# Convolution taps, map differences and RoPE on VectorE in a two-layer hybrid attention block

## The chip, the cores and the metric

The kernel runs on one core of one Trainium2 chip. The metric is the device time of one execution in microseconds (us), the median of several runs. A core has five engines with queues of their own: PE (TensorE, matmuls; its weight loads are listed as PEld), DVE (VectorE), ACT (ScalarE), POOL (GpSimd) and SP (SyncE, which issues the DMAs here). PE writes its results to PSUM; everything else lies in SBUF.

## The reference, cut to what matters

512 latent tokens and 256 context tokens of width 1024 go through two layers. A layer normalises and modulates its input, projects it to 2560 columns in one combined projection, and computes four head groups from that; their outputs are joined, projected and added to the stream, and a SwiGLU feed-forward network follows. The second layer computes no context output. What the change touches:

```python
def apply_rope(x, cos, sin):                      # groups A and C, latent tokens only
    x1, x2 = x[..., :half], x[..., half:]
    return concatenate([x1 * cs - x2 * sn, x1 * sn + x2 * cs])

def conformer_conv(u, w_dw, b_dw, ln_g, ln_b):    # group B: 256 channels
    a, gate = split(u, 2)
    h = a * sigmoid(gate)
    h = depthwise_conv(h, w_dw, taps=31, padding=15) + b_dw
    return silu(layernorm(h, ln_g, ln_b))

def diff_weights(q, k, v, lam):                   # group C: 4 heads, 2 maps each, 32 columns
    p = softmax(q k^T * 32 ** -0.5)
    w = p[map 0] - lam * p[map 1]
    return w @ v
```

Group A is windowed attention with a sink, group D neighbourhood attention on an 8 x 64 grid.

## The kernel before, in words

All matmuls of weights are done in three passes (`mm3`): each operand is held as a high part (fp32r) and a low part, and the products high-high, high-low and low-high are summed in PSUM. A weight tile (`w_unit`) is loaded by SP into one of three raw buffers (wraw), cast to its high part by ACT (whi, L142) and its low part is subtracted by DVE or, for some units, by POOL (wlo, L144). A projection of 128 columns (`unit`) writes the 512 latent tokens and, where needed, the 256 context tokens into the two PSUM buffers pu. While `self.half` is 1 the latent tokens are done as two passes of 256 columns each, behind the context tokens; otherwise as one pass of 512, ahead of them. `self.half` is 1 from the start of group C's attention to the end of group A's projections: in each layer q and k of the second half of group C, q, k and v of group D, and four units of group A.

`rope` (L466) copies a projection out of PSUM on ACT, swaps the halves with a matmul by a permutation (into PSUM, pt), multiplies by sine and cosine on DVE (L474, L475) and adds the two on POOL (L476). There are seven in each layer, four of group C and three of group A.

The convolution (`conv_taps`, L871) runs per half of the channels, 128 channels on the partitions and 783 columns in layer 0 (latent tokens, padding, context) or 512 in layer 1. Of the 31 taps, 20 are formed on ACT as a scaled copy (cpr, L885; the first one, L882, is written to accp directly) and added on POOL (accp, L886); 11 are done on DVE as a multiply and an add in one instruction (accd, L892 and L894). POOL adds both sums at the end (yB, L897). It is a generator: each step is one tap of POOL and about half a tap of DVE, and `mix2` draws steps between those of other generators, in the projections of groups B, C and D. The space of the convolution is given back before the value projections of group D.

`c_attn` (L634) works through blocks of 128 queries and one head: twelve blocks for each of the two head pairs in layer 0 (eight latent ones with 768 keys, four of context with 256), eight in layer 1. A block computes the scores of both maps (sc, L628; there is one score buffer), reduces each to its smallest value while it moves it to SBUF (Pm, nm, L660, DVE), exponentiates on ACT (L663), computes the coefficient (cf, L668, DVE), and takes the weighted difference of the maps: in layer 1 and in every second block of layer 0 as a scaling on ACT (L671) and an addition on POOL (L672), else in one instruction on DVE (L674). The result is transposed on PE (pt, L513) and copied out (PT, L524 on ACT, L527 on DVE); `evac` shares such copies out by the columns given to each engine so far. PE then multiplies by V (L619).

`beside` runs a main generator with a side one between its steps. Group C's first pair runs beside the rest of the projections of group C and the first ones of D, its second pair beside the remaining ones of D.

The program gives an order, and a planner (`schedule_with_timeline_sim=True`) puts the instructions of each engine in their final order by its own costs; each engine then works through its queue in order.

Of the kernel before, what the change touches and what calls it, by code (L numbers as in the profile page):

```python
# [10 lines left out]
AF = mybir.ActivationFunctionType  # L11
ALU = mybir.AluOpType
# [4 lines left out]
P = 128  # L17
D = 1024
NK = D // P
SEQ = 512  # L20
CTX = 256
NT = SEQ + CTX
# [12 lines left out]
QSC_AD = -0.125  # L35
QSC_C = -(32.0 ** -0.5)
CONV_K = 31
CONV_P = 20
PADC = 15
HPW = PADC + SEQ + PADC + CTX + PADC  # L40
ACW = SEQ + PADC + CTX
# [9 lines left out]
class Hybrid:  # L51
# [414 lines left out]
    def rope(self, lat, ct, st, pm, pool):  # L466

        nc = self.nc
        e = self.tl(pool, [P, 512], "rt", 4)
        nc.scalar.copy(e, lat[:, 0:512])  # L470
        sw = self.ps("pt")
        nc.tensor.matmul(sw[:, 0:512], self.perm[:, pm * P:(pm + 1) * P], e, start=True, stop=True)
        v = self.tl(pool, [P, 512], "rt", 4)
        nc.vector.tensor_tensor(v, sw[:, 0:512], self.cs[:, st:st + 512], op=ALU.mult)  # L474
        nc.vector.tensor_tensor(e, e, self.cs[:, ct:ct + 512], op=ALU.mult)  # L475
        nc.gpsimd.tensor_tensor(e, e, v, op=ALU.add)  # L476
        return e

    QKB = 12
# [39 lines left out]
    def evac(self, dst, src):  # L519

        n = int(np.prod(src.shape[1:]))
        if self.load[0] <= self.load[1] * 2.0:
            self.load[0] += n
            self.nc.scalar.copy(dst, src)  # L524
        else:
            self.load[1] += n
            self.nc.vector.tensor_copy(dst, src)  # L527
# [107 lines left out]
    def c_attn(self, l, u):  # L635
        nc = self.nc
        q_ = self.lay[l]
        if u == 0:
            self.nblk = 0
            self.L0 = self.tl(self.cpool, [P, 6, 4], "L0", 1)  # L640
        L0 = self.L0
        Q, K = self.qkc["q", u], self.qkc["k", u]
        for n in range(6 if l == 0 else 4):
            lat = n < 4
            w = NT if lat else CTX
            nb = w // P
            PT = []
            for j in range(2):
                h = 2 * u + j
                rows = [slice(64 * j + 32 * m, 64 * j + 32 * m + 32) for m in range(2)]  # L650
                pss = self.ps2("sc")
                qs = [[a[:, n * P:(n + 1) * P] for a in Q]] * 2
                self.burst_of([f for c0, c1, o in (((0, 512, 0), (512, NT, 512)) if lat else ((512, NT, 0),)) for f in
                               self.mm_rows([ps[:, o:o + c1 - c0] for ps in pss], qs, [[a[:, c0:c1] for a in K]] * 2, rows)])
                Pm = []
                lm = self.small(1, "l1")
                for m in range(2):
                    nm = self.small(1, "nm")
                    Pm.append(self.a_s())
                    nc.vector.tensor_tensor_reduce(out=Pm[m][:, 0:w], in0=pss[m][:, 0:w],  # L660
                                                   in1=self.zcol.to_broadcast([P, w]),
                                                   scale=1.0, scalar=HUGE, op0=ALU.add, op1=ALU.min, accum_out=nm)
                    nc.scalar.activation(Pm[m][:, 0:w], Pm[m][:, 0:w], AF.Exp, scale=-1.0, bias=nm,  # L663
                                         accum_out=L0[:, n, h:h + 1] if m == 0 else lm)
                rl = self.small(1, "rl")
                nc.vector.reciprocal(rl, lm)
                cf = self.small(1, "cf")
                nc.vector.scalar_tensor_tensor(cf, L0[:, n, h:h + 1], q_["nlam"], rl, op0=ALU.mult, op1=ALU.mult)  # L668
                self.nblk += 1
                if l or self.nblk % 2 == 0:  # L670
                    nc.scalar.activation(Pm[1][:, 0:w], Pm[1][:, 0:w], AF.Copy, scale=cf)  # L671
                    nc.gpsimd.tensor_tensor(Pm[0][:, 0:w], Pm[0][:, 0:w], Pm[1][:, 0:w], op=ALU.add)  # L672
                else:
                    nc.vector.scalar_tensor_tensor(Pm[0][:, 0:w], Pm[1][:, 0:w], cf, Pm[0][:, 0:w],  # L674
                                                   op0=ALU.mult, op1=ALU.add)
                PT.append(self.a_pt())
                self.tr_copy([Pm[0][:, b * P:(b + 1) * P] for b in range(nb)], PT[j])
                yield
            self.pv([[(self.VC[:, kb, (2 * u + j) * 64:(2 * u + j) * 64 + 64], self.blk(PT[j], kb - 6 + nb))
                      for kb in range(6 - nb, 6)] for j in range(2)], self.yg["C"][:, u, n * P:(n + 1) * P])  # L680
# [190 lines left out]
    def conv_taps(self, l, pool, u):  # L871
        nc = self.nc
        w = ACW if l == 0 else SEQ
        acc = self.tl(self.cv, [P, ACW], "accd", 1)
        hp = self.hp[u]
        accp = self.tl(self.cv, [P, ACW], "accp", 1)
        nv = CONV_K - CONV_P
        for k in range(CONV_P):
            wc = self.wcol[:, l * 62 + 2 * k + u:l * 62 + 2 * k + u + 1]
            src = hp[:, k:k + w]  # L880
            if k == 0:
                nc.scalar.activation(accp[:, 0:w], src, AF.Identity, scale=wc, bias=self.vcol[:, 2 * l + u:2 * l + u + 1])  # L882
            else:
                pr = self.tl(self.cv, [P, ACW], "cpr", 2)
                nc.scalar.activation(pr[:, 0:w], src, AF.Copy, scale=wc)  # L885
                nc.gpsimd.tensor_tensor(accp[:, 0:w], accp[:, 0:w], pr[:, 0:w], op=ALU.add)  # L886
            for j in range(k * nv // CONV_P, (k + 1) * nv // CONV_P):
                kk = CONV_P + j
                wc = self.wcol[:, l * 62 + 2 * kk + u:l * 62 + 2 * kk + u + 1]
                src = hp[:, kk:kk + w]  # L890
                if j == 0:
                    nc.vector.tensor_scalar(acc[:, 0:w], src, wc, None, op0=ALU.mult)  # L892
                else:
                    nc.vector.scalar_tensor_tensor(acc[:, 0:w], src, wc, acc[:, 0:w], op0=ALU.mult, op1=ALU.add)  # L894
            yield
        for a0, a1, c0 in ((0, SEQ, 0), (SEQ, NT, ACW - CTX))[:1 if l else 2]:
            nc.gpsimd.tensor_tensor(self.yg["B"][:, u, a0:a1], accp[:, c0:c0 + a1 - a0], acc[:, c0:c0 + a1 - a0],  # L897
                                    op=ALU.add)

    def conv_norm(self, l, pool):  # L900
        nc = self.nc
# [102 lines left out]
    def layer(self, l):  # L1004
# [77 lines left out]
        self.cv = self.pool("conv", "left")  # L1082
        self.VC = self.tl(c1, [P, 6, 256], "V", 1)
        self.VA = self.tl(c1, [P, 6, P], "VA", 1)
        self.load = [0, 0]

        def taps():
            for u in range(2):
                yield from self.conv_taps(l, c1, u)
        tp = taps()  # L1090
        for u in range(2):
            for _ in self.mix2(self.proj_b(l, H, c1, u), tp if u else iter(()), 1, False):
                pass
        self.burst, self.ada_tag, self.atags = 0, "pt", [("wraw", 3, F32, self.wst)]
        adas = self.ada_gen([(0, 3)] if l == 0 else [])
        for _ in self.mix2(self.mix2(self.proj_c(l, H, c1, 0), tp, 3, False), adas, 2, False):
            pass
        for _ in adas:
            pass
# [2 lines left out]
        nq = 6 if cx else 4  # L1102

        def d_rest():
            yield from self.mix2(self.proj_d(l, H, c1, 1), tp, 5, False)
            for _ in tp:
                pass
            self.cv.release()
            c2 = held["c2"] = self.pool("mixd", "left")
            self.VD = self.tl(c2, [P, 6, 256], "VD", 1)  # L1110
            self.maskd = self.tl(c2, [P, 768], "mask")
            self.dma(self.maskd, t["maskd"])
            for u in range(2):
                self.v_turned(self.unit(self.w_unit(t["w_in"][l], DV + u * P, True), H, True, "k"), c1,
                              self.VD[:, :, u * P:(u + 1) * P])
                yield
# [11 lines left out]
        def more():  # L1128
# [2 lines left out]
            both = [self.load_wo(l, wo, held["wop"], range(wa)), self.ada_gen([(l, 2)])]  # L1131
            yield from self.chain(*both[::-1 if l else 1])

        self.half = 1
        self.beside(self.c_attn(l, 0), self.mix2(self.chain(self.proj_c(l, H, c1, 1), self.proj_d(l, H, c1, 0)), tp, 4, False),
                    2 * nq, 4)
        self.beside(self.c_attn(l, 1), d_rest(), 2 * nq, 4)
        self.psum_pop()
        self.psum_push("e")
        dn = 10 if cx else 8  # L1140
# [196 lines left out]
def _constants():  # L1337
# [5 lines left out]
    for dim, cc, ss in ((64, C_CA, C_SA), (32, C_CC, C_SC)):  # L1343
        nf = dim // 4
        inv = (np.float32(10000.0) ** (-np.arange(nf, dtype=np.float32) / np.float32(nf))).astype(np.float32)
        ang = np.concatenate([row[:, None] * inv, col[:, None] * inv], axis=1)
        p = np.arange(P)
        idx = p % (dim // 2)
        sgn = np.where(p % dim < dim // 2, -1.0, 1.0).astype(np.float32)
        c[:, cc:cc + SEQ] = np.cos(ang).astype(np.float32).T[idx]  # L1350
        c[:, ss:ss + SEQ] = np.sin(ang).astype(np.float32).T[idx] * sgn[:, None]
        perm[p, 0 if dim == 64 else 1, p ^ (dim // 2)] = 1.0
# [39 lines left out]
```

## Time and profile before

| what | value |
|---|---|
| median of 3 runs | 1831.48 us (1829.79 to 1834.33) |
| profiled execution | 1833.57 us |
| its span, first to last instruction | 1831.8 us |
| mean granted TensorE clock | 0.974 of full speed |
| busy in the span: PE, DVE, ACT, POOL | 1722.9, 904.9, 673.9, 435.0 us |

Busy time is the union of the times in which an engine has an instruction in work. Matmuls are pipelined, so a busy PE is not PE at its peak. The granted clock is that of TensorE, 1.0 being 2.4 GHz and 0.5 being 1.2 GHz; a value between is a mean over a stretch. The waits are idle time of an engine, put down to the instruction that ended last before it could go on. In the rows, `out<-in` are the program's own tile names.

### The profile page before, as it was taken

Reading aid. Unit: us, or ns where it says so; the run is one execution under the profiler, and the core shown is the slowest. Engines: PE = TensorE matmul, PEld = TensorE weight load, DVE = VectorE, ACT = ScalarE, POOL = GpSimd, SP = SyncE. Lnnn points to the kernel's source line nnn. Section 1 sums busy time; section 2 is a strip of 40 time slices with the busy share of each in tenths; the row PEclk is TensorE's granted clock in tenths of the full one; section 3 lists DMA queues with packets and bytes.
Section 4 is the critical chain, followed back from the end, with each engine's and each line's share of the span. In section 5 each row is a group of like instructions: output and inputs, shape, how many; then the busy total and the mean of one; then the engine's idle time right before and its main releaser. Section 6 shows DMA issues by size and latency. Waiting matters only on the chain.

```text
span 1831.8 us, 28387 instructions
## 1 busy us (share of the span) xinstructions
PE 1722.9 (94%) x11812; PEld 1456.6 (80%) x11812; DVE 904.9 (49%) x1435; ACT 673.9 (37%) x1161; POOL 435.0 (24%) x324
## 2 busy tenths in 40 slices
PE   6987999878999999999999999899988999999997
PEld 4776888666898778888888888779966888888886
DVE  4668753664362442332424358654366445444354
ACT  4355664653151112121121236576455232221322
POOL 1488723331000010000000015893351000000002
PEclk8998999988999999999999999999989999999999
DMA  9341201306124444234231211121224163323321
GB/s 319 86 130 41 61 24 55 104 24 209 62 79 145 128 140 128 83 104 129 70 95 40 88 69 58 47 55 37 77 72 150 58 207 92 104 81 92 115 70 46
DMA packets 187983, 172.88 MB, mean 94 GB/s; under 512 B 17878, under 2 KB 150478, under 8 KB 187726
## 3 DMA queue, kind: packets, MB, share of 16 engines
q1 hardware_dynamic: 187854, 171.06, 30.4%
q8 instruction: 93, 1.52, 0.4%
q14 instruction: 36, 0.29, 0.0%
HBM read 166.76 MB, written 4.52 MB: 94 GB/s over the span
## 4 chain that ended last, share of the span: by engine, by line
PE 75%; DVE 7%; POOL 6%; issue 3%; DMA 3%; ACT 3%; SPq 2%; POOLq 0%; ACTq 0%; DVEq 0%
PE ps L177 18%; PE ps L178 18%; PE ps L179 18%; POOL accp L886 4%; PE pu L178 3%; PE pu L177 3%; PE pu L179 3%; PE pt L513 2%; PE pt L619 2%; SPq L98 2%; PE sc L628 2%; PE ada L307 2%; DVE accd L894 1%; PE pu L619 1%; DVE wlo L144 1%
## 5 line engine op out<-in xcount | busy, mean ns | idle before, releaser
L178 PE MATMUL ps<-h,whi 128*128 128x512 f32 (+1 forms) x1104 | 384.0, 349 | 2.5 <-DVE h L144 2.5
L177 PE MATMUL ps<-h,whi 128*128 128x512 f32 (+1 forms) x1104 | 383.0, 349 | 0.9 <-DVE gt L993 0.9
L179 PE MATMUL ps<-h,wlo 128*128 128x512 f32 (+1 forms) x1104 | 383.4, 348 | 0.0
L142 ACT CAST whi<-wraw 128x1024 fp32r<-128x1024 f32 (+1 forms) x132 | 134.3, 1021 | 413.3 <-PE ps L178 249.3
L144 DVE TENSOR_TENSOR wlo<-wraw,whi 128x1024 fp32r<-128x1024 f32 (+1 forms) x116 | 149.0, 1289 | 205.2 <-ACT whi L142 204.0
L178 PEld LDWEIGHTS ps<-h,whi 128*128 128x128 f32 x1104 | 209.5, 190 | 30.0 <-DVE h L144 3.2
L177 PEld LDWEIGHTS ps<-h,whi 128*128 128x128 f32 x1104 | 208.4, 190 | 29.8 <-issue 2.6
L179 PEld LDWEIGHTS ps<-h,wlo 128*128 128x128 f32 x1104 | 209.5, 190 | 27.3 <-issue 2.0
L177 PE MATMUL pu<-hT,whi 128*128 128x256 f32 (+1 forms) x648 | 197.0, 304 | 8.2 <-DVE qk L147 3.3
L996 POOL TENSOR_TENSOR x<-x,gt 128x1024 f32<-128x1024 f32 x12 | 29.7, 2474 | 731.2 <-DVE gt L993 731.2
L179 PE MATMUL pu<-hT,wlo 128*128 128x256 f32 (+1 forms) x648 | 193.9, 299 | 0.0
L178 PE MATMUL pu<-hT,whi 128*128 128x256 f32 (+1 forms) x648 | 193.7, 299 | 0.0
L177 PE MATMUL ps<-wdhi,zh 128*128 128x512 f32 x440 | 171.7, 392 | 0.4 <-ACT ntmp L382 0.4
L178 PE MATMUL ps<-wdlo,zh 128*128 128x512 f32 x440 | 171.0, 390 | 0.0
L179 PE MATMUL ps<-wdhi,zl 128*128 128x512 f32 x440 | 170.4, 391 | 0.0
L993 DVE TENSOR_TENSOR gt<-ps,g 128x1024 f32<-128x1024 f32 x66 | 80.6, 1222 | 148.9 <-PE ps L179 129.8
L886 POOL TENSOR_TENSOR accp<-accp,cpr 128x783 f32<-128x783 f32 (+1 forms) x76 | 145.6, 1915 | 19.8 <-ACT cpr L885 13.9
L142 ACT CAST wdhi<-wraw 128x1024 fp32r<-128x1024 f32 x44 | 46.1, 1052 | 271.5 <-PE ps L179 181.1
L177 PEld LDWEIGHTS pu<-hT,whi 128*128 128x128 f32 x648 | 123.9, 191 | 17.0 <-DVE qk L147 3.8
L178 PEld LDWEIGHTS pu<-hT,whi 128*128 128x128 f32 x648 | 124.1, 191 | 5.7 <-issue 2.4
L179 PEld LDWEIGHTS pu<-hT,wlo 128*128 128x128 f32 x648 | 124.2, 192 | 5.1 <-issue 2.2
L1259 DVE TENSOR_TENSOR sg<-sg,ps 128x768 f32<-128x768 f32 (+1 forms) x44 | 36.1, 820 | 143.8 <-PE ps L179 123.0
(270 smaller groups left out, 2964.3 us busy)
## 6 DMA issues: line engine op xcount, KB each, us to landing
araw<-in_w_ada SPq DMA_DIRECT2D x60, 512.0 KB
wraw<-in_w_gate SPq DMA_DIRECT2D x44, 512.0 KB
wraw<-in_w_up SPq DMA_DIRECT2D x44, 512.0 KB
wraw<-in_w_down SPq DMA_DIRECT2D x44, 512.0 KB
wraw<-in_w_in SPq DMA_DIRECT2D x40, 512.0 KB
wraw<-in_w_ada SPq DMA_DIRECT2D x20, 512.0 KB
wraw<-in_w_out SPq DMA_DIRECT2D x12, 512.0 KB
whi<-in_w_ada SPq DMA_DIRECT2D x8, 512.0 KB
```

The lines of the kernel that those rows point to most:

```text
L98: self.nc.sync.dma_start(out, in_)
L142: nc.scalar.copy(hi, src)
L144: eng.tensor_tensor(lo, src, f32(hi), op=ALU.subtract)
L177: mm(out, st[0], mv[0], start=first, stop=False)
L178: mm(out, st[0], mv[1], start=False, stop=False)
L179: mm(out, st[1], mv[0], start=False, stop=last)
L307: nc.tensor.matmul(ps[32 * j:32 * j + 32, 0:P], self.cstat[:, k, :], raw[:, a * 512 + j * P:a * 512 + (j + 1) * P], start=(k == 0), stop=( ...
L513: self.nc.tensor.transpose(pt[:, (i - a) * P:(i - a + 1) * P], blocks[i], self.ident)
L619: self.burst_of([lambda i=i, j=j: nc.tensor.matmul(po[64 * j:64 * j + 64, 0:P], *parts[j][i], start=(i == n - 1), stop=(i == 0)) for i in ...
L628: return [lambda o=o, q=q[a][r], k=k[b][r], i=i: self.nc.tensor.matmul(o, q, k, start=(i == 0), stop=(i == 2)) for i, (a, b) in enumerate( ...
L886: nc.gpsimd.tensor_tensor(accp[:, 0:w], accp[:, 0:w], pr[:, 0:w], op=ALU.add)
L993: nc.vector.tensor_tensor(tmp, ps, g, op=ALU.mult)
```

## The change

- `rope`: no copy on ACT. DVE multiplies the projection in PSUM by sine and by cosine; the permutation matmul is applied to the sine product (the constant signs are swapped accordingly), and DVE adds its PSUM result to the cosine product. POOL has no part in it.
- `conv_taps`: the first tap and the bias on ACT, taps 1 to 29 on DVE in one accumulator, the last tap on DVE straight into the output tile, in one piece in layer 1 and two in layer 0. A step is now one tap.
- `c_attn`: the map difference is one DVE instruction in all blocks.
- `evac`: while `act_evac` is set (from the start of a layer's mixer until the taps are done) all such copies go to ACT.
- `self.half` is 0 throughout: latents are projected 512 columns at a time.
- Taps are drawn at other places: three per step of the second half of group B's projection, six per step of group C's first projections, then one (layer 0) or two (layer 1) behind each block of `c_attn`; none in the later projections. What is left is issued ahead of the value projections of group D.

```diff
     def rope(self, lat, ct, st, pm, pool):
-        e = self.tl(pool, [P, 512], "rt", 4)
-        nc.scalar.copy(e, lat[:, 0:512])
+        e, v = (self.tl(pool, [P, 512], "rt", 4) for _ in range(2))
+        nc.vector.tensor_tensor(v, lat[:, 0:512], self.cs[:, st:st + 512], op=ALU.mult)
+        nc.vector.tensor_tensor(e, lat[:, 0:512], self.cs[:, ct:ct + 512], op=ALU.mult)
         sw = self.ps("pt")
-        nc.tensor.matmul(sw[:, 0:512], self.perm[:, pm * P:(pm + 1) * P], e, start=True, stop=True)
-        v = self.tl(pool, [P, 512], "rt", 4)
-        nc.vector.tensor_tensor(v, sw[:, 0:512], self.cs[:, st:st + 512], op=ALU.mult)
-        nc.vector.tensor_tensor(e, e, self.cs[:, ct:ct + 512], op=ALU.mult)
-        nc.gpsimd.tensor_tensor(e, e, v, op=ALU.add)
+        nc.tensor.matmul(sw[:, 0:512], self.perm[:, pm * P:(pm + 1) * P], v, start=True, stop=True)
+        nc.vector.tensor_tensor(e, sw[:, 0:512], e, op=ALU.add)
         return e
...
     def evac(self, dst, src):
-        if self.load[0] <= self.load[1] * 2.0:
+        if self.act_evac or self.load[0] <= self.load[1] * 2.0:
...
     def c_attn(self, l, u):
-                self.nblk += 1
-                if l or self.nblk % 2 == 0:
-                    nc.scalar.activation(Pm[1][:, 0:w], Pm[1][:, 0:w], AF.Copy, scale=cf)
-                    nc.gpsimd.tensor_tensor(Pm[0][:, 0:w], Pm[0][:, 0:w], Pm[1][:, 0:w], op=ALU.add)
-                else:
-                    nc.vector.scalar_tensor_tensor(Pm[0][:, 0:w], Pm[1][:, 0:w], cf, Pm[0][:, 0:w],
-                                                   op0=ALU.mult, op1=ALU.add)
+                nc.vector.scalar_tensor_tensor(Pm[0][:, 0:w], Pm[1][:, 0:w], cf, Pm[0][:, 0:w],
+                                               op0=ALU.mult, op1=ALU.add)
...
     def conv_taps(self, l, pool, u):
-        accp = self.tl(self.cv, [P, ACW], "accp", 1)
-        nv = CONV_K - CONV_P
-        for k in range(CONV_P):
+        for k in range(CONV_K):
             wc = self.wcol[:, l * 62 + 2 * k + u:l * 62 + 2 * k + u + 1]
-            src = hp[:, k:k + w]
             if k == 0:
-                nc.scalar.activation(accp[:, 0:w], src, AF.Identity, scale=wc, bias=self.vcol[:, 2 * l + u:2 * l + u + 1])
+                nc.scalar.activation(acc[:, 0:w], hp[:, 0:w], AF.Identity, scale=wc,
+                                     bias=self.vcol[:, 2 * l + u:2 * l + u + 1])
+            elif k < CONV_K - 1:
+                nc.vector.scalar_tensor_tensor(acc[:, 0:w], hp[:, k:k + w], wc, acc[:, 0:w], op0=ALU.mult, op1=ALU.add)
             else:
-                pr = self.tl(self.cv, [P, ACW], "cpr", 2)
-                nc.scalar.activation(pr[:, 0:w], src, AF.Copy, scale=wc)
-                nc.gpsimd.tensor_tensor(accp[:, 0:w], accp[:, 0:w], pr[:, 0:w], op=ALU.add)
-            for j in range(k * nv // CONV_P, (k + 1) * nv // CONV_P):
...
+                for a0, a1, c0 in ((0, SEQ, 0), (SEQ, NT, ACW - CTX))[:1 if l else 2]:
+                    c1 = c0 + a1 - a0
+                    nc.vector.scalar_tensor_tensor(self.yg["B"][:, u, a0:a1], hp[:, k + c0:k + c1], wc, acc[:, c0:c1],
+                                                   op0=ALU.mult, op1=ALU.add)
             yield
...
     def layer(self, l):
-        self.load = [0, 0]
+        self.load, self.act_evac = [0, 0], True
...
-            for _ in self.mix2(self.proj_b(l, H, c1, u), tp if u else iter(()), 1, False):
+            for _ in self.mix2(self.proj_b(l, H, c1, u), tp if u else iter(()), 3, False):
...
-        for _ in self.mix2(self.mix2(self.proj_c(l, H, c1, 0), tp, 3, False), adas, 2, False):
+        for _ in self.mix2(self.mix2(self.proj_c(l, H, c1, 0), tp, 6, False), adas, 2, False):
...
         def d_rest():
-            yield from self.mix2(self.proj_d(l, H, c1, 1), tp, 5, False)
+            yield from self.proj_d(l, H, c1, 1)
             for _ in tp:
                 pass
             self.cv.release()
+            self.act_evac = False
...
-        self.half = 1
-        self.beside(self.c_attn(l, 0), self.mix2(self.chain(self.proj_c(l, H, c1, 1), self.proj_d(l, H, c1, 0)), tp, 4, False),
-                    2 * nq, 4)
-        self.beside(self.c_attn(l, 1), d_rest(), 2 * nq, 4)
+        self.half = 0
+        self.beside(self.mix2(self.c_attn(l, 0), tp, 1 + l, False),
+                    self.chain(self.proj_c(l, H, c1, 1), self.proj_d(l, H, c1, 0)), 2 * nq, 4)
+        self.beside(self.mix2(self.c_attn(l, 1), tp, 1 + l, False), d_rest(), 2 * nq, 4)
```

## Rows read from the trace of the kernel before

**Rows 1.** The chain that ended last, by line, of the page: shares of the span.
```profile
PE ps L177 18%; PE ps L178 18%; PE ps L179 18%; POOL accp L886 4%; PE pu L178 3%; PE pu L177 3%; PE pu L179 3%; PE pt L513 2%; PE pt L619 2%; SPq L98 2%; PE sc L628 2%; PE ada L307 2%; DVE accd L894 1%; PE pu L619 1%; DVE wlo L144 1%
```

**Rows 2.** Stretches: start:end, length, busy us of each engine, granted clock, DMA share, GB/s.
```profile
72.00:235.00 163.00, 140.86 (x1157) 123.63 (x1156) 125.19 (x164) 93.95 (x158) 128.48 (x71) 0.95 0.27 76
134.00:205.00 71.00, 59.48 (x491) 53.39 (x490) 62.40 (x76) 43.63 (x72) 63.68 (x30) 0.93 0.15 44
260.00:340.00 80.00, 79.61 (x722) 70.85 (x720) 34.01 (x100) 39.84 (x104) 24.36 (x29) 1.00 0.18 53
1119.00:1240.00 121.00, 108.31 (x826) 96.13 (x825) 85.96 (x116) 79.76 (x132) 104.20 (x71) 0.97 0.22 61
```

**Rows 3.** Waits of PE, 72 to 235 us: total us, times, longest.
```profile
PE pt L513 <- DVE Pm L674: 10.7, 1, 10.7
PE pu L177 <- DVE qk L147: 3.3, 1, 3.3
PE sc L628 <- DVE nm L660: 2.6, 3, 1.3
...
PE pu L178 <- DVE wlo L144: 1.3, 1, 1.3
```

**Rows 4.** Waits of PE, 1119 to 1240 us.
```profile
PE sc L628 <- DVE nm L660: 4.1, 1, 4.1
PE pu L177 <- DVE qk L144: 2.6, 1, 2.6
PE pu L177 <- ACT rt L470: 1.7, 1, 1.7
PE pt L472 <- ACT rt L470: 1.6, 1, 1.6
```

**Rows 5.** Chain in order of time, 138 to 165 us: start, us, what.
```profile
150.97 1.71 DVE cf L668
152.68 3.12 DVE accd L894
```

**Rows 6.** Single lines, 72 to 235 and 1119 to 1240 us: duration ns min/median/max.
```profile
L894 DVE SCALAR_TENSOR_TENSOR accd<-hp,wcol,accd x20: 1022/2508/3193, 77.5 to 163.6; 128x783 f32<-128x783 f32 x20
...
L894 DVE SCALAR_TENSOR_TENSOR accd<-hp,wcol,accd x20: 740/1668/1777, 1121.7 to 1177.7; 128x512 f32<-128x512 f32 x20
...
L668 DVE SCALAR_TENSOR_TENSOR cf<-L,nlam,rl x14: 219/402/1785, 150.9 to 233.8; 128x1 f32<-128x1 f32 x14
...
L144 DVE TENSOR_TENSOR wlo<-wraw,whi x6: 1235/2368/2860, 72.5 to 137.3; 128x1024 fp32r<-128x1024 f32 x6
```

**Rows 7.** DVE groups, 72 to 235 us: count, busy us, mean ns, idle before.
```profile
L894 DVE SCALAR_TENSOR_TENSOR accd<-hp,wcol,accd 128x783 f32<-128x783 f32 x20 | 41.2, 2061 | 0.4
...
L144 DVE TENSOR_TENSOR wlo<-wraw,whi 128x1024 fp32r<-128x1024 f32 x6 | 13.9, 2310 | 21.8 <-ACT whi L142 21.8
L674 DVE SCALAR_TENSOR_TENSOR Pm<-Pm,cf,Pm 128x768 f32<-128x768 f32 x5 | 10.4, 2088 | 0.1
L668 DVE SCALAR_TENSOR_TENSOR cf<-L,nlam,rl 128x1 f32<-128x1 f32 x14 | 10.2, 727 | 0.5
```

**Rows 8.** The single line L672, 1119 to 1240 us.
```profile
L672 POOL TENSOR_TENSOR Pm<-Pm,Pm x9: 1812/1841/2304, 1178.8 to 1236.2; 128x768 f32<-128x768 f32 x9
```

**Rows 9.** Timeline of PE, from 95 and from 249 us: start, us, instruction.
```profile
94.82 0.40 PE L177 MATMUL pu<-hT,whi 128*128 128x512 f32 x1
...
98.78 0.40 PE L179 MATMUL pu<-hT,wlo 128*128 128x512 f32 x1
...
249.84 0.28 PE L177 MATMUL pu<-hT,whi 128*128 128x256 f32 x1
...
251.16 0.28 PE L179 MATMUL pu<-hT,wlo 128*128 128x256 f32 x1
```

**Rows 10.** The single lines L474 and L475, 72 to 235 us.
```profile
L474 DVE TENSOR_TENSOR rt<-pt,cst x4: 673/680/684, 101.4 to 191.7; 128x512 f32<-128x512 f32 x4
...
L475 DVE TENSOR_TENSOR rt<-rt,cst x4: 678/966/1162, 102.4 to 192.3; 128x512 f32<-128x512 f32 x4
```

More of the change, by code (lines that the diff above doesn't have):

```diff
@@ L37 @@
 CONV_K = 31
-CONV_P = 20
 PADC = 15
@@ L638, in c_attn @@
         if u == 0:
-            self.nblk = 0
             self.L0 = self.tl(self.cpool, [P, 6, 4], "L0", 1)
@@ L875, in conv_taps @@
         hp = self.hp[u]
-        accp = self.tl(self.cv, [P, ACW], "accp", 1)
-        nv = CONV_K - CONV_P
-        for k in range(CONV_P):
+        for k in range(CONV_K):
             wc = self.wcol[:, l * 62 + 2 * k + u:l * 62 + 2 * k + u + 1]
-            src = hp[:, k:k + w]
             if k == 0:
-                nc.scalar.activation(accp[:, 0:w], src, AF.Identity, scale=wc, bias=self.vcol[:, 2 * l + u:2 * l + u + 1])
-            else:
-                pr = self.tl(self.cv, [P, ACW], "cpr", 2)
-                nc.scalar.activation(pr[:, 0:w], src, AF.Copy, scale=wc)
-                nc.gpsimd.tensor_tensor(accp[:, 0:w], accp[:, 0:w], pr[:, 0:w], op=ALU.add)
-            for j in range(k * nv // CONV_P, (k + 1) * nv // CONV_P):
[L888 to L894, printed above, removed]
+                nc.scalar.activation(acc[:, 0:w], hp[:, 0:w], AF.Identity, scale=wc,
+                                     bias=self.vcol[:, 2 * l + u:2 * l + u + 1])
+            elif k < CONV_K - 1:
+                nc.vector.scalar_tensor_tensor(acc[:, 0:w], hp[:, k:k + w], wc, acc[:, 0:w], op0=ALU.mult, op1=ALU.add)
+            else:
+                for a0, a1, c0 in ((0, SEQ, 0), (SEQ, NT, ACW - CTX))[:1 if l else 2]:
+                    c1 = c0 + a1 - a0
+                    nc.vector.scalar_tensor_tensor(self.yg["B"][:, u, a0:a1], hp[:, k + c0:k + c1], wc, acc[:, c0:c1],
+                                                   op0=ALU.mult, op1=ALU.add)
             yield
-        for a0, a1, c0 in ((0, SEQ, 0), (SEQ, NT, ACW - CTX))[:1 if l else 2]:
-            nc.gpsimd.tensor_tensor(self.yg["B"][:, u, a0:a1], accp[:, c0:c0 + a1 - a0], acc[:, c0:c0 + a1 - a0],
-                                    op=ALU.add)
     def conv_norm(self, l, pool):
@@ L1348, in _constants @@
         idx = p % (dim // 2)
-        sgn = np.where(p % dim < dim // 2, -1.0, 1.0).astype(np.float32)
+        sgn = np.where(p % dim < dim // 2, 1.0, -1.0).astype(np.float32)
         c[:, cc:cc + SEQ] = np.cos(ang).astype(np.float32).T[idx]
```

## Prediction

> **What bounds the kernel now.** I read the page first, then a table of stretches, then what the matmul engine waits for in the stretches that the change touches. The chain of waits is mostly matmuls, but two of its entries belong to the edited lines: the POOL additions of the convolution (accp, 4%) and its VectorE taps (accd, 1%) [rows 1]. The table shows where PE isn't full. In layer 0, from the first tap to the middle of the second half of group C (72 to 235 us), PE is busy 140.9 of 163 us, 22.1 idle; in layer 1 (1119 to 1240 us) 108.3 of 121, 12.7 idle. POOL and DVE are as busy as PE there: from 134 to 205 us POOL 63.7 and DVE 62.4 of 71. From 260 to 340 us PE is full (79.6 of 80) [rows 2], so nothing that only shortens another engine counts there.
>
> The waits name who ended the idle time. Layer 0: 10.7 us once for a map difference on DVE (Pm L674), 3.3 for a RoPE result (qk L147), 2.6 for the reductions that free the score buffer (nm L660), 1.3 for a weight split (wlo L144) [rows 3], 17.9 in all. Layer 1: 4.1 for the reductions, 2.6, 1.7 and 1.6 around RoPE [rows 4], 10.0 in all. The chain through the 10.7 us is DVE alone: the one-column coefficient cf took 1.71 us, the tap behind it 3.12 [rows 5]. Undisturbed they are short. Taps of 783 columns run from 1.02 to 3.19 us with a median of 2.51, taps of 512 columns from 0.74 with a median of 1.67, cf from 0.22 to 1.79 [rows 6]; in the timeline the short ones are those with POOL at rest. So DVE instructions and POOL's additions hold each other up, and what PE waits for stands behind them.
>
> **The change part by part.**
>
> *Taps.* In each layer POOL loses 38 additions and the final sums and ACT 38 scalings; VectorE has 60 taps in place of 22. Undisturbed, that is 60 x 1.02 = 61 us in layer 0 and 60 x 0.74 = 44 in layer 1 [rows 6]. Does DVE hold that? Of its 125.2 us busy in 72 to 235 [rows 2], today's taps are 41.2, and the excess over the undisturbed length is 13.9 - 6 x 1.24 = 6.5 in six weight splits, 10.4 - 5 x 1.02 = 5.3 in five map differences (a pass like a tap's over 768 columns), 10.2 - 14 x 0.22 = 7.1 in 14 coefficients [rows 6, 7]. 65 us remain. I add 61 for taps, 5 for six map differences that come from POOL (four of 768 columns, two short), 3 for a third RoPE operation in four RoPEs, and take off about 5 for evacuations that go to ACT: 129 us. Some eight taps (8 us) will come after 235 us, since the second half of group C draws one per step. So 121 us of DVE beside some 137 us of PE work (163 less 22 idle and 4 of clock): close, but under it. In layer 1 the taps are shorter and there is more room.
>
> *Map difference.* In every layer-1 block and half of layer 0's it is now a scaling on ACT and a POOL addition of 1.84 us [rows 8]; on DVE it is one instruction of about 1.02. The probabilities come a microsecond sooner or more.
>
> *Waits that go.* All eight of [rows 3, 4] end in DVE behind a held instruction, in POOL's queue (the RoPE sum stands behind accp), or in ACT behind a scaling that waits for POOL. I count them all: 27.9 us. What is late next is a weight that has just landed, and its cast; the 34.8 us of idle time less these 27.9 leave 6.9 for such waits, which I leave standing.
>
> *Clock.* The granted clock was 0.95 over 163 us and 0.97 over 121 [rows 2]: 8.2 + 3.6 = 11.8 us of full-speed time lost if PE had been busy throughout. Part of the low spells lies under idle time and cost nothing. Between 0 and 12 I take 6, the middle.
>
> *512 columns at a time.* Two passes of 256 become one in 12 projections of each layer (two of group C, four query and key and two value ones of group D, four of group A), 24 pairs each: 576 pairs. Eleven steps between starts of 256 columns take 1.32 us (0.120 each), seventeen of 512 take 3.96 (0.233) [rows 9]: 0.007 us a pair, 4 us. Bounds: nothing, and 7.
>
> *RoPE from PSUM.* A copy on ACT and a sum on POOL go; DVE does three operations, each with one operand in PSUM. Such an operation took 0.67 to 0.68 us whatever POOL did, the one with both inputs in SBUF 0.68 to 1.16 [rows 10]. The path to q or k gets shorter by about the POOL sum. The projection's PSUM buffer is held for two operations (1.36 us) before it is free, under the next projection's matmuls; I cost it at nothing, and without that cover it would be at most 1.36 us for each of 14 RoPEs, 19 us.
>
> *Evacuations.* Transposed maps of group C go to ACT, which loses its scalings; afterwards the balance sends evacuations to DVE until it has caught up. From 260 to 340 us DVE is free for 46 of 80 us [rows 2], which hides them; without that cover a dozen copies of 512 columns like the 0.68 us operations of [rows 10] are 8 us.
>
> *What is added.* The score buffer is single: the next block's scores wait until DVE has reduced both halves, and now one tap per block (layer 1: two) is drawn into DVE's queue around those reductions. Below: nothing, if the taps fall into DVE's pauses. Above: each block pays its taps, about 19 x 1.02 in layer 0 and 26 x 0.74 in layer 1, 39 us. The nearest rows are the waits for these reductions now, 2.6 + 4.1 = 6.7 us [rows 3, 4]; DVE stays as full as it was, so I take 9.
>
> One rule speaks against the change. In the trace a tap held by POOL takes 2.51 us instead of 1.02 [rows 6]. The Trainium skill, SBUF — State Buffer, section "Who interferes with whom", says that a VectorE instruction with two SBUF inputs and a GpSimd instruction that reads SBUF exclude each other for a whole instruction. The held taps agree with it; by it the weight splits that stay on POOL (seven in this stretch of layer 0) would each still hold a tap, some 7 x 1.5 = 10 us of DVE time, and the sum would come out about 3 us later than without it.
>
> *Sum.* 27.9 + 6 + 4 - 9 = 29 us off. The profiled execution took 1833.57 us (span 1831.8, 1.8 around it), so 1804.6; it lay 2.1 above the median of the runs, 1831.48, so about 1802 for the median.
>
> **Rivals.**
> *Weights are late next.* With DVE free, the projections wait for the load, cast and split of the next weight, through a ring of three raw buffers. For it: the waits for qk and wlo stand in front of projections [rows 3, 4]. Against: the DMA engines are busy 0.27 and 0.22 of the time [rows 2]. Then 3.3 + 1.3 + 2.6 + 1.7 + 1.6 stay, and half of the clock's 6: 13.5 us less gained, 1816.
> *DVE becomes the bound: slower.* The place is DVE's queue ahead of the two reductions of each group C block. If each block pays its taps (39) and the splits left on POOL hold DVE for 10 more, 49 stand against 38 gained: 1842. It decides from 38 us, 0.85 us for each of the 45 taps. For it: 121 us of DVE in 137. Against it: PE has projections to fill with while scores wait.
> *It does not relieve.* The order of instructions on each engine comes from a planner; it could put the taps under what is left on POOL, so that they stay long. Then only the wider projections count: 1827. Against: only the splits and the small bias tiles of group D are left on POOL there.
>
> **How the numbers follow.** Forecast 0.62 (own range 1788 to 1816), weights 0.20, no relief 0.04, DVE as the bound 0.14, of which 0.05 ends near no change. A measurement of this kernel can't tell less than 0.3% (5.5 us) from no change: faster 0.62 + 0.20 = 0.82, same 0.04 + 0.05 = 0.09, slower 0.09. The low end takes no new waits and the upper bounds of clock and passes, 29 + 9 + 6 + 3 = 47: 1785. The high end takes in the weights and no relief, and the lighter case of DVE: 1829.
>
> **What would show it.** Right: taps of 783 columns near 1.03 us in the median and cf near 0.22; no wait of PE over 3 us in group C; POOL mostly idle from 72 to 235 us; the clock at 1.0 there; starts 0.23 us apart in the projections of groups A, C and D. Wrong: PE waiting for reductions for more than 15 us in all, DVE over nine tenths busy with PE idle beside it, or taps that stay at twice their length.

## The result and the profile after

The changed kernel takes 1810.1 us in the median of four runs (1805.92 to 1812.19), beside 1831.17 for the kernel before: a ratio of 0.988 with a 95% interval of 0.9858 to 0.9901. So it is 21 us faster, inside the predicted range, where the forecast had 29. The profiled execution took 1809.8 us (span 1808.0), 23.8 us less than the profiled one of before.

The page's busy times of the changed kernel: VectorE has taken over the work (941.5 us for 904.9), POOL keeps half of its 435.0, ScalarE loses 88.

```profile
PE 1715.8 (95%) x11236; PEld 1415.6 (78%) x11236; DVE 941.5 (52%) x1546; ACT 586.3 (32%) x1052; POOL 216.8 (12%) x200
```

The chain of waits by line, which answers to [rows 1]. The POOL additions (accp, 4%) are gone from it; the VectorE taps (accd) stand there with 3% in place of 1%.

```profile
PE ps L176 19%; PE ps L177 19%; PE ps L178 19%; PE pu L176 4%; PE pu L178 4%; PE pu L177 4%; DVE accd L873 3%; PE pt L616 2%; PE sc L625 2%; PE pt L510 2%; PE ada L306 2%; PE pu L616 1%; DVE Pm L656 1%; SPq L97 1%; DMA araw<-in_w_ada 1%
```

The stretches of [rows 2] in the changed kernel (the last one 9 us earlier, as the kernel is by then); columns as there.

```profile
72.00:235.00 163.00, 151.79 (x1097) 124.69 (x1097) 135.18 (x215) 62.14 (x129) 23.20 (x19) 0.96 0.28 79
134.00:205.00 71.00, 63.24 (x418) 50.87 (x417) 64.62 (x103) 29.16 (x63) 16.46 (x16) 0.90 0.17 44
260.00:340.00 80.00, 73.93 (x585) 57.53 (x583) 49.65 (x128) 35.52 (x91) 19.25 (x25) 0.99 0.24 74
1110.00:1230.00 120.00, 116.99 (x757) 95.44 (x756) 103.66 (x167) 50.65 (x96) 22.66 (x18) 0.99 0.24 65
```

PE's idle time falls from 22.1 to 11.2 us in the first stretch and from 12.7 to 3.0 in the last. But in the second the granted clock went down, from 0.93 to 0.90. The third is not the same work any more: it lies 8 us further on in the kernel, where the small bias and probability tiles of group D are still POOL's.

What PE waits for from 72 to 235 us, which answers to [rows 3] (total us, times, longest):

```profile
PE pt L510 <- DVE Pm L665: 6.6, 4, 4.7
PE pu L176 <- DVE hp L587: 2.2, 1, 2.2
PE sc L625 <- DVE nm L656: 0.9, 1, 0.9
PE pu L176 <- ACT qk L581: 0.9, 1, 0.9
```

and from 1110 to 1230 us, where one row is left of [rows 4]:

```profile
PE sc L625 <- DVE nm L656: 3.0, 3, 1.0
```

The waits for RoPE and for the weight split are gone, and those for the reductions (nm) fell from 6.7 to 3.9 us. One that begins at the map difference (Pm) is still there: 4.7 us in one piece, where it was 10.7.

The single lines that answer to [rows 6], between 60 and 340 us and, for the second tap row, in layer 1 (duration in ns min/median/max):

```profile
L873 DVE SCALAR_TENSOR_TENSOR accd<-hp,wcol,accd x58: 1007/1029/2797, 78.1 to 189.8; 128x783 f32<-128x783 f32 x58
...
L873 DVE SCALAR_TENSOR_TENSOR accd<-hp,wcol,accd x58: 733/752/2850, 1112.2 to 1192.6; 128x512 f32<-128x512 f32 x58
...
L664 DVE SCALAR_TENSOR_TENSOR cf<-L,nlam,rl x24: 211/219/1836, 134.7 to 286.3; 128x1 f32<-128x1 f32 x24
...
L665 DVE SCALAR_TENSOR_TENSOR Pm<-Pm,cf,Pm x24: 476/1012/3094, 136.3 to 286.6; 128x768 f32<-128x768 f32 x16, 128x256 f32<-128x256 f32 x8
```

Medians of taps fell from 2508 and 1668 ns to 1029 and 752: the typical tap has its undisturbed length. The maxima did not fall: something still holds a few.

What the remaining 4.7 us is made of stands in the chain from 160 to 176 us (start, us, what):

```profile
162.54 0.87 DVE Pm L656
163.41 0.01 DVE nm L656
163.42 0.96 DVE accd L873
164.38 0.02 issue
164.40 1.03 DVE accd L873
165.43 0.07 DVE rl L662
165.51 1.00 DVE accd L873
166.50 0.13 DVE cf L664
166.63 0.94 DVE accd L873
167.58 3.02 DVE Pm L665
170.60 0.14 issue
170.74 1.10 PE pt L510 x4
```

PE has nothing to do from about 166.0 us on. The chain it waits for is all DVE: two taps ahead of the reciprocal rl, one between rl and the coefficient cf, one between cf and the map difference, and then the map difference itself at three times its median, 3.02 us. VectorE's timeline has a second long instruction a little earlier, a tap,

```profile
154.85 2.80 DVE L873 SCALAR_TENSOR_TENSOR accd<-hp,wcol,accd 128x783 f32<-128x783 f32 x1
```

and POOL's names what runs beside the two: two weight splits.

```profile
154.34 2.47 POOL L143 TENSOR_TENSOR wlo<-wraw,whi 128x1024 fp32r<-128x1024 f32 x1 [14.77 <-ACT whi L141]
...
167.10 2.67 POOL L143 TENSOR_TENSOR wlo<-wraw,whi 128x1024 fp32r<-128x1024 f32 x1 [10.29 <-ACT whi L141]
```

Each long instruction starts behind its split, at 154.85 and 167.58; the tap at 166.63, which starts ahead of the second split, has its usual length.

In ten-microsecond stretches (columns as in [rows 2]):

```profile
150.00:160.00 10.00, 10.00 (x74) 8.15 (x74) 10.00 (x15) 3.97 (x9) 2.47 (x1) 1.00 0.17 52
160.00:170.00 10.00, 4.66 (x38) 3.93 (x36) 9.96 (x13) 4.50 (x9) 2.67 (x1) 0.90 0.00 0
170.00:180.00 10.00, 9.02 (x45) 6.27 (x46) 9.93 (x19) 3.73 (x9) 0.00 (x0) 0.50 0.18 54
180.00:190.00 10.00, 10.00 (x57) 8.29 (x56) 7.30 (x13) 3.67 (x8) 0.00 (x0) 0.92 0.00 0
```

DVE is full up to 180 us. PE pauses from 160 to 170, and through the ten microseconds after that the granted clock is 0.50, the lower of the two levels, 1.2 GHz, though PE is at work again.

### The profile page after: what moved, and what is told of

Read it like the earlier page. It is cut to its first block, busy times and chain, and to the rows that moved or that the text cites. A ratio compares the mean times of both kernels' runs of the same rounds, so it can differ in the third digit from the quotient of the medians.

```text
span 1808.0 us, 26990 instructions
## 1 busy us (share of the span) xinstructions
PE 1715.8 (95%) x11236; PEld 1415.6 (78%) x11236; DVE 941.5 (52%) x1546; ACT 586.3 (32%) x1052; POOL 216.8 (12%) x200
## 4 chain that ended last, share of the span: by engine, by line
PE 81%; DVE 9%; DMA 4%; ACT 2%; issue 2%; POOL 1%; SPq 1%; POOLq 0%; ACTq 0%; DVEq 0%
PE ps L176 19%; PE ps L177 19%; PE ps L178 19%; PE pu L176 4%; PE pu L178 4%; PE pu L177 4%; DVE accd L873 3%; PE pt L616 2%; PE sc L625 2%; PE pt L510 2%; PE ada L306 2%; PE pu L616 1%; DVE Pm L656 1%; SPq L97 1%; DMA araw<-in_w_ada 1%
## 5 line engine op out<-in xcount | busy, mean ns | idle before, releaser
L143 DVE TENSOR_TENSOR wlo<-wraw,whi 128x1024 fp32r<-128x1024 f32 (+1 forms) x116 | 140.1, 1211 | 199.0 <-ACT whi L141 198.0
L176 PE MATMUL pu<-hT,whi 128*128 128x512 f32 (+1 forms) x456 | 163.2, 358 | 4.8 <-DVE hp L587 2.2
L177 PE MATMUL pu<-hT,whi 128*128 128x512 f32 (+1 forms) x456 | 160.7, 353 | 0.0
L178 PE MATMUL pu<-hT,wlo 128*128 128x512 f32 (+1 forms) x456 | 160.5, 352 | 0.0
L873 DVE SCALAR_TENSOR_TENSOR accd<-hp,wcol,accd 128x783 f32<-128x783 f32 (+1 forms) x116 | 112.8, 972 | 2.8 <-ACT accd L870 1.2
L176 PEld LDWEIGHTS pu<-hT,whi 128*128 128x128 f32 x456 | 86.5, 190 | 21.0 <-issue 2.6
L176 PEld LDWEIGHTS ps<-wdhi,zh 128*128 128x128 f32 x440 | 82.6, 188 | 19.3 <-issue 1.4
L178 PEld LDWEIGHTS pu<-hT,wlo 128*128 128x128 f32 x456 | 86.8, 190 | 12.7 <-issue 1.8
```

The source lines that it names most:

```text
L143: eng.tensor_tensor(lo, src, f32(hi), op=ALU.subtract)
L176: mm(out, st[0], mv[0], start=first, stop=False)
L177: mm(out, st[0], mv[1], start=False, stop=False)
L178: mm(out, st[1], mv[0], start=False, stop=last)
L873: nc.vector.scalar_tensor_tensor(acc[:, 0:w], hp[:, k:k + w], wc, acc[:, 0:w], op0=ALU.mult, op1=ALU.add)
```

## Experiments

Each kernel was timed beside the kernel before on the same chip, whose medians there were 1834.3, 1833.62 and 1832.96 us in the three groups; so ratios are compared, not times. "Changed" is the changed kernel.

**Which part carries the gain.** e2_taps_alone is the kernel before with the taps on VectorE and the places where they are drawn, and nothing else of the change; e3_taps_back is the changed kernel with the taps, their draws and the evacuations as before.

```diff
 e2_taps_alone against before
-        for k in range(CONV_P):
+        for k in range(CONV_K):
...
-                nc.scalar.activation(pr[:, 0:w], src, AF.Copy, scale=wc)
-                nc.gpsimd.tensor_tensor(accp[:, 0:w], accp[:, 0:w], pr[:, 0:w], op=ALU.add)
+                nc.vector.scalar_tensor_tensor(acc[:, 0:w], hp[:, k:k + w], wc, acc[:, 0:w], op0=ALU.mult, op1=ALU.add)
...
-        self.beside(self.c_attn(l, 1), d_rest(), 2 * nq, 4)
+        self.beside(self.mix2(self.c_attn(l, 1), tp, 1 + l, False), d_rest(), 2 * nq, 4)

 e3_taps_back: the same lines the other way, in the changed kernel, and
-        self.load, self.act_evac = [0, 0], True
+        self.load, self.act_evac = [0, 0], False
```

> The kernel before, with only the taps changed (all on VectorE, drawn where the change draws them); RoPE, map differences, evacuations and 256-column passes as before. Theory (the taps' POOL additions were what held DVE): most of the gain is here, 1813 to 1822. Rival (map difference and RoPE are what PE waited for, the taps only add work to DVE): 1828 or more.

> The complement: RoPE, map differences and wide passes as changed, but the taps shared out between ACT, POOL and VectorE and drawn as before, evacuations as before. Theory: POOL's additions still hold DVE, so the long taps stay (median near 2.5 us in layer 0) and less than half of the gain is left, 1820 to 1828. Rival (map difference and RoPE carry the gain): 1815 or less.

Measured: taps alone 1815.48 us, 0.9897 [0.9881, 0.9913], 19 us faster than before. Everything but the taps and the evacuations: 1836.9 us, 1.0016 [1.0006, 1.0027], 3 us slower. The first came out as the theory had it; for the second both ideas were wrong, as each had it faster. The interval of e2_taps_alone overlaps that of the changed kernel, so what the rest of the change adds to the taps is not clear of noise. And e2_taps_alone is more than POOL's relief: ACT loses 38 scalings a layer, and the taps are drawn at other places. No run takes these apart; of PE's waits before, 7.8 us ended directly in ACT in the two stretches of [rows 3, 4].

The trace of e3_taps_back says why nothing is left. The single line of its taps, from 72 to 235 us:

```profile
L886 DVE SCALAR_TENSOR_TENSOR accd<-hp,wcol,accd x20: 1034/2497/2998, 77.3 to 158.3; 128x783 f32<-128x783 f32 x20
```

PE's waits in the same stretch:

```profile
PE pt L473 <- DVE rt L470: 11.2, 2, 6.9
PE pt L511 <- DVE mcol L326: 5.8, 1, 5.8
```

and its chain of waits from 92 to 100 us, where the longer of the two waits at L473 ends:

```profile
92.52 2.50 DVE accd L886
95.02 0.02 issue
95.04 2.49 DVE accd L886
97.53 0.61 DVE rt L470
98.14 0.04 issue
98.19 2.08 PE pt L473 x2
```

With POOL still adding, a tap takes 2.5 us, and the first RoPE product, which is now DVE's, stands behind two of them, while PE waits for it. RoPE from PSUM is free only behind short taps: the parts of the change are not terms that can be added.

**What POOL still holds up.** e4_wlo_dve takes the weight splits that POOL still does in the changed kernel to VectorE.

```diff
-            eng = nc.gpsimd if pool else nc.vector
+            eng = nc.vector
```

> The changed kernel with the weight splits that stayed on POOL put on VectorE too. Theory (what is left of waits in layer 0, 6.6 us for Pm and a fall of the clock, is again DVE held by POOL, at 154 and 167 us): DVE instructions of 2.8 to 3.1 us go, the wait with them, 1800 to 1807. Rival (DVE is simply full from 130 to 180 us, so that any work more on it costs): 8 splits of 1.22 us make it 5 to 10 us slower than the changed kernel, 1815 to 1820.

Measured: 1798.97 us, 0.9818 [0.9797, 0.9838]: another 11 us. The single line of its taps, from 60 to 340 us:

```profile
L873 DVE SCALAR_TENSOR_TENSOR accd<-hp,wcol,accd x58: 1015/1030/1036, 76.6 to 189.4; 128x783 f32<-128x783 f32 x58
```

PE's two longest waits from 72 to 235 us:

```profile
PE pu L176 <- DVE hp L587: 1.9, 1, 1.9
PE pt L510 <- DVE Pm L665: 1.4, 1, 1.4
```

and its map differences:

```profile
L665 DVE SCALAR_TENSOR_TENSOR Pm<-Pm,cf,Pm x24: 477/1012/1019, 136.6 to 278.9; 128x768 f32<-128x768 f32 x16, 128x256 f32<-128x256 f32 x8
```

The longest tap is 1.036 us and the longest map difference 1.019, where they were 2.797 and 3.094: none is held any more, and the wait at the map difference has fallen from 6.6 to 1.4 us. In layer 1 the 3.0 us of waits for the reductions are gone. DVE has more to do and PE waits less for it. This is the plainest showing that the splits on POOL made those instructions long.

**Columns at a time, and the order of the columns.** `self.half` brings two edits at once: with 1 the latent columns go in two passes of 256, and the 256 context columns go first, not behind them. e1_half sets it back in the changed kernel, e5_wide_alone sets it to 0 in the kernel before, e6_wlo_half sets it to 1 with the splits on VectorE. e8_ctx_first and f1_wlo_ctx_first keep 512 columns and put the context first (changed kernel, and with the splits on VectorE); f4_wlo_half_lat has passes of 256 with the latent columns first and the splits on VectorE.

```diff
 e1_half, e6_wlo_half (e5_wide_alone the other way, in before)
-        self.half = 0
+        self.half = 1

 e8_ctx_first, f1_wlo_ctx_first
-            groups.insert(0 if split_lat else 1, (ctx, CTX0, CTX0 + 256))
+            groups.insert(0, (ctx, CTX0, CTX0 + 256))

 f4_wlo_half_lat
-            groups.insert(0 if split_lat else 1, (ctx, CTX0, CTX0 + 256))
+            groups.append((ctx, CTX0, CTX0 + 256))
```

> The kernel after the change, but latents projected as two passes of 256 columns again in the 12 later projections of each layer. Theory (the gain is the release of DVE from POOL's additions; wide passes are a small term): 4 us slower than the changed kernel, 1814, at most 1818. Rival (the wide passes, with 576 fewer matmuls and loads for PE, are the main part of the 21 us): 1822 or more.

> The kernel before with one edit: latents projected 512 columns at a time. Theory (a pass of 512 is a coarser filler between the steps of attention, and PE waits at the joints for it; it costs by itself): 2 to 8 us slower than before. Rival 1 (the 0.007 us a pair that the prediction counted): 4 us faster. Rival 2 (the cost seen with the changed kernel belongs to its own order of instructions): within 2 us of before.

> The changed kernel with all weight splits on VectorE and passes of 256 columns. Theory (two separate causes: DVE held by POOL's splits, PE waiting at the joints of wide passes): both gains add, about 1793. Rival (both edits mend the same waits of layer 0 and layer 1): no faster than the splits alone, 1797 to 1801.

> The changed kernel, 512 columns at a time, but the context tokens of each projection ahead of the latent ones, as the narrow passes have it. Theory (width): no better than the changed kernel, 1808 to 1813. Rival (the narrow form was faster for its order: the context part covers the wait for the buffer of the latent part): 1804 to 1806.

> The changed kernel with all weight splits on VectorE, 512 columns at a time, context tokens first. Of the four cases of width and order it is the wide one in the order of the narrow one. Theory (order: the context part first is what helped): like the narrow one with these splits, 1784 to 1791. Rival (width): like the wide one with latents first, 1796 to 1801.

> All weight splits on VectorE, 256 columns at a time, but latent tokens first. Theory (order): as slow as the wide one with latents first, 1796 to 1801. Rival (width): as fast as the narrow one with context first, 1784 to 1790.

Measured, as ratios to before (median us):

| base | 512, latent first | 512, context first | 256, context first | 256, latent first |
|---|---|---|---|---|
| before | 1.0010 [1.0, 1.0019] (1835.68) | - | 1 | - |
| changed | 0.988 [0.9858, 0.9901] (1810.1) | 0.9817 [0.9802, 0.9832] (1801.07) | 0.9836 [0.982, 0.9852] (1804.06) | - |
| changed, splits on VectorE | 0.9818 [0.9797, 0.9838] (1798.97) | 0.9834 [0.9818, 0.985] (1802.34) | 0.9746 [0.9733, 0.9759] (1786.53) | 0.9791 [0.9776, 0.9805] (1795.58) |

Three pairs differ in the width alone. With the splits on VectorE 512 columns cost 16 us with the context first and 5, at the edge of the noise, with the latent first; in the changed kernel with the context first 512 columns are 3 us faster in the medians, but the two intervals overlap. In two pairs the order changes along: 512 columns cost 8 us in the changed kernel, and 2, at the edge of the interval, in the kernel before. No pair shows a gain clear of noise. Three pairs differ in the order alone. The context first gains 12 us in the changed kernel at 512 columns and 8 with the splits on VectorE at 256; at 512 columns with those splits it is 3 us slower, with overlapping intervals. So the 8 us of e1_half need no width: e8_ctx_first keeps 512 columns, turns the order alone, and gains more.

Of the ideas, both of e1_half fell, as each had 256 columns slower. e5_wide_alone came out at its second rival's limit of 2 us; the 4 us of the first are not there. e6_wlo_half has both gains, and 6 us more than the theory gave it. e8_ctx_first is faster than either idea had it. f1_wlo_ctx_first went with width, its rival, and f4_wlo_half_lat lies between its two, 5 us below the wide kernel and 8 above the narrow one with the context first.

e6_wlo_half is the fastest kernel of the study, 47 us below the kernel before and 24 below the changed one. Its table from 150 to 190 us, beside the one above:

```profile
150.00:160.00 10.00, 10.00 (x96) 8.89 (x96) 10.00 (x17) 4.64 (x11) 0.00 (x0) 1.00 0.19 54
160.00:170.00 10.00, 10.00 (x87) 8.97 (x88) 10.00 (x17) 5.42 (x11) 0.00 (x0) 1.00 0.13 39
170.00:180.00 10.00, 10.00 (x95) 9.45 (x90) 10.00 (x18) 5.25 (x11) 0.00 (x0) 1.00 0.05 15
180.00:190.00 10.00, 10.00 (x96) 9.01 (x95) 10.00 (x17) 4.65 (x11) 0.00 (x0) 1.00 0.19 54
```

DVE is as full as in the changed kernel, but PE has projection work to put into every pause, and the clock stays at its upper level. So a full DVE is no bound by itself. Why the planner's order leaves PE without work at 166 us in the one kernel and not in the other was not found.

**Evacuations and a control.** e7_evac_shared is the changed kernel with the evacuations shared as before; f2_wlo_half_evac does the same to e6_wlo_half; f3_swap takes the two first RoPE products in the other order, which should do nothing.

```diff
 e7_evac_shared, f2_wlo_half_evac
-        self.load, self.act_evac = [0, 0], True
+        self.load, self.act_evac = [0, 0], False

 f3_swap
-        nc.vector.tensor_tensor(v, lat[:, 0:512], self.cs[:, st:st + 512], op=ALU.mult)
         nc.vector.tensor_tensor(e, lat[:, 0:512], self.cs[:, ct:ct + 512], op=ALU.mult)
+        nc.vector.tensor_tensor(v, lat[:, 0:512], self.cs[:, st:st + 512], op=ALU.mult)
```

> The changed kernel with the copies out of PSUM shared out between ACT and DVE throughout. Theory (DVE is full from 130 to 180 us in layer 0, so a third of the copies on it costs): 3 to 8 us slower than the changed kernel, 1813 to 1818. Rival (the later imbalance, where DVE takes nearly all copies in group D, costs as much as it saves): 1808 to 1811, or faster.

> The kernel with all weight splits on VectorE, 256 columns at a time and context first, and the copies out of PSUM shared out between ACT and DVE throughout. Theory (sending all copies to ACT, and then nearly all to DVE in group D, costs 7 us of itself): 1778 to 1783. Rival (the 7 us seen in the changed kernel came from its order of instructions, which missed a collision with a POOL split): 1785 to 1792.

> The changed kernel with the two products of RoPE issued in the other order (cosine first), an edit with no price of its own worth 1 us. Theory (differences of 5 to 9 us between such kernels are real causes): within 3 us of the changed kernel, 1807 to 1813. Rival (the planner's order of instructions falls out differently with any edit, and each order meets or misses collisions of a POOL split with a DVE instruction that PE waits for): more than 4 us away, either way.

Measured: e7_evac_shared 1803.08 us, 0.9837 [0.9823, 0.985], about 8 us faster than the changed kernel where the theory had it slower; f2_wlo_half_evac 1795.42, 0.979 [0.9774, 0.9806], about 8 us slower than e6_wlo_half; f3_swap 1810.74, 0.9872 [0.9855, 0.9888], the same as the changed kernel. e7_evac_shared went the way of its rival, f2_wlo_half_evac went the way of its rival and lies 3 us beyond its range, and f3_swap came out as its theory had it. The evacuations matter by some 8 us, with a sign that depends on the rest. f3_swap is one small edit that does not shuffle the time; it does not show that none does.

## Why the prediction was right, and where its sizes were off

The time can be split by PE itself. The rows are the mixer of each layer, of before, of the changed kernel, of e4_wlo_dve and of e6_wlo_half: from 72 us, and in layer 1 from the first projection of that mixer, up to the first matmul of the output projection.

```profile
72.00:434.70 362.70, 317.42 (x2830) 271.10 (x2828) 240.41 (x479) 206.36 (x434) 194.43 (x134) 0.94 0.24 71
1099.80:1401.70 301.90, 275.64 (x2417) 241.99 (x2417) 180.08 (x358) 180.88 (x339) 173.72 (x136) 0.97 0.20 59
```

```profile
72.00:426.80 354.80, 317.35 (x2542) 253.80 (x2540) 253.17 (x536) 161.20 (x379) 75.38 (x73) 0.94 0.25 72
1090.70:1380.50 289.80, 272.67 (x2129) 221.50 (x2129) 205.48 (x413) 139.75 (x286) 75.43 (x73) 0.98 0.21 62
```

```profile
72.00:420.20 348.20, 316.87 (x2540) 252.88 (x2538) 251.28 (x544) 160.72 (x379) 56.73 (x63) 0.94 0.25 74
1083.70:1368.50 284.80, 272.02 (x2129) 221.36 (x2129) 205.33 (x422) 141.38 (x287) 53.90 (x65) 0.98 0.22 65
```

```profile
72.00:415.70 343.70, 313.80 (x2830) 268.92 (x2828) 250.62 (x543) 160.81 (x378) 54.47 (x63) 0.96 0.25 75
1079.50:1357.90 278.40, 268.98 (x2417) 236.43 (x2417) 205.48 (x420) 138.22 (x285) 55.13 (x65) 0.99 0.22 64
```

Length less PE's busy time is its idle time: 45.3 + 26.3 = 71.5 us before, 37.5 + 17.1 = 54.6 after. So 17.0 us came from idle time and 3.0 from busy time (593.1 to 590.0); 3.8 of the 23.8 lie elsewhere in the kernel, and the experiments did not look there.

- **Waits that go, less new waits (27.9 - 9 = 18.9 us).** Measured 17.0 of idle time: the size is right, its make-up is not. Of the eight waits five are gone; those at the map difference and at the reductions only shrank, from 10.7 to 6.6 and from 6.7 to 3.9 us. These 10.5 us stand beside the 9, but the 9 were taps drawn ahead of the reductions. With the splits on VectorE too, and the taps drawn as before, e4_wlo_dve has 1.6 us left at the same two places (1.4 and 0.2), so most of the 10.5 goes with the splits. That the two sums agree is in part luck.
- **Where the gain is.** Not as expected: layer 0, with 17.9 of the 27.9 us, gained 7.9, layer 1 12.1. In layer 0 DVE has a tap of 1.03 us per draw and is full from 150 to 180 us; in layer 1 a tap is 0.75 and DVE has room, 103.7 of 120 us. That this is the reason is not shown: in e6_wlo_half DVE is as full there, and the mixer of layer 0 is 19.0 us shorter than before.
- **The clock (6 us).** Half right at most. In layer 1 the mean went from 0.97 to 0.98, and by the clock records the time at 1.2 GHz fell from 20.5 to 10.2 us, worth up to half of that, 5. In layer 0 it stayed at 0.94 (41.1 and 40.4 us at 1.2 GHz). In the two stretches from which the 6 were taken it fell from 23.9 to 17.1 us, worth 3.4 at most. The pause of 4.7 us from 166 on lies together with 13.7 us at that clock (168.0 to 181.7): the sum counted the waits and the clock apart, and here a wait that stays stands beside a clock that stays low.
- **512 columns (4 us).** The step that failed. PE's busy time fell by 3.0 us in all, no more than the clock can have given, and no pair of experiments shows a gain clear of noise from the wider pass. The price per pair was too high: over the two mixers of the changed kernel, passes of 512 start 0.233 us apart in the median and passes of 256 columns 0.118, so a pair gives 0.003 us and not 0.007, and 576 pairs 1.7 us and not 4. The run of 256 columns in [rows 9], at 0.120, was a little slower than most. Why 512 columns cost up to 16 us in some pairs is argued only: in a stretch where PE has pauses, a shorter stream of matmuls leaves it without work sooner. No run shows that by itself.
- **RoPE (nothing).** Right with short taps: no wait for it is left in the rows above. It rested on the taps: with them held, e3_taps_back waits 11.2 us for the first product.
- **Evacuations (nothing, 8 at most).** The bound was right, the value wrong: sharing them is worth 8 us in the changed kernel and costs 8 in e6_wlo_half.
- **The splits left on POOL (10 us of DVE, 3 of the sum).** The mechanism was right and its price in time too low. In the stretch of the seven splits three taps, one map difference and two coefficients of the changed kernel are held, for 8.4 us beyond their usual lengths. Taking the splits off POOL shortened the mixer of layer 0 by 6.6 us, not 3, and that of layer 1, for which the prediction gave no price, by 5.0. Of these 11.6 us 10.5 are idle time of PE, and 8.2 of them are the fall of the waits at the map difference (6.6 to 1.4) and of layer 1's at the reductions (3.0 to none). The clock has little part in it: the time at 1.2 GHz is 40.9 and 9.6 us, beside 40.4 and 10.2. The Trainium skill, SBUF — State Buffer, section "Who interferes with whom", has a VectorE instruction with two SBUF inputs and a GpSimd instruction that reads SBUF exclude each other; e4_wlo_dve agrees, with the longest tap at 1.036 us and no POOL instruction from 67 to 198 us, in which all the taps lie. One reading of the prediction was too simple: in layer 0 of the kernel before, the short taps are not only those with POOL at rest. Three of the seven short ones have a POOL addition that starts 0.1 to 0.5 us behind them; the long ones are those that start while POOL is already at one.

Of the rivals, "weights are late next" did not come: no wait for a split is left in the rows. "No relief" is refuted by the medians of the taps. "DVE becomes the bound" is half there: its sign, DVE over nine tenths busy with PE idle beside it, shows from 160 to 170 us, at 5 us of idle time and not at the 49 it was priced. Of the signs named, those for taps, cf, POOL (23.2 us of 163) and the starts of 0.23 us came; "no wait over 3 us" came in layer 1 and failed in layer 0, with 4.7; the clock from 72 to 235 us was 0.96 and not 1.0.

What stays open: why the effects of pass width, column order and evacuations change size or sign with what stands beside them, by up to 16 us, which is not far from the whole gain of 21. The planner's order differs among these kernels, and no run held that order fixed while changing one of them.

## What to carry to other kernels

When two engines lengthen each other's instructions, move all of the one's work in that stretch and not most of it: here the last eight splits of each layer were worth 11 us, more than half of the 19 that moving the taps gave. Price the parts of a change together where one stands in the other's queue: PE did not wait for RoPE on DVE behind taps of 1 us, and waited 11 us for it behind taps of 2.5. Take the price of a pass from the median of many starts: eleven steps in one place gave 0.007 us a pair, the median 0.003.

## What was not expected of the hardware

A pause of 4.7 us of PE, with DVE full, and 13.7 us at 1.2 GHz from 168.0 us on lie together in the changed kernel; for 10.9 us of them PE was at work again, and at half the clock these lose up to 5.4 us, somewhat more than the wait itself. The length of the pause alone does not give that of the spell: in e4_wlo_dve, with a wait of 1.4 us that ended at 164.4, the clock was at 1.2 GHz for 6.9 us from 164.2 on. And DVE fully busy for 40 us beside PE fully busy for the same 40 us (e6_wlo_half, 150 to 190 us) shows no slowing of either there: its taps have the length they have alone, 1.03 us, and PE's passes of 256 columns start 0.119 us apart in the median, 0.118 over the whole mixer. In two neighbouring rows the start told which instruction is held: in the changed kernel a tap that began 0.5 us ahead of a POOL split took 1.03 us, and the map difference that began 0.5 us behind it 3.02.
